# Third filter layer in two 64-row halves, and convolution-tap spectra in 32-row groups, in a diffusion trunk kernel

## Chip, cores and metric

One core of one Trainium2 chip. The metric is the device time of one execution in microseconds (us); lower is better. Engines: TensorE (PE; its weight loads are PEld), VectorE (DVE), ScalarE (ACT), GpSimd (POOL); SyncE (SP) issues most transfers.

## What is computed

Two trunk layers on 128 context tokens and 256 latent tokens of width 1024 in fp32. The parts that matter here are the filters of the long convolution and the taps of the depthwise convolution:

```python
def hyena_filters(L, w1, b1, f1, w2, b2, f2, w3, log_decay):
    ...
    h = jnp.sin(f1 * (z @ w1 + b1))
    h = jnp.sin(f2 * (h @ w2 + b2))
    h = (h @ w3).reshape(L, HYENA_ORDER, 2, HYENA_W)      # third layer: 64 -> 2 orders x 512
    decay = jnp.exp(log_decay).reshape(HYENA_ORDER, 2, HYENA_W)
    h = h * jnp.exp(-tn[:, None, None, None] * decay[None])
    return h * lax.rsqrt(jnp.sum(h * h, axis=(0, 2), keepdims=True) + EPS)

def trunk_layer(x, cond, l, P, cache):
    mod = (silu(cond) @ P['w_mod'][l] + P['b_mod'][l])     # nine modulation vectors
    h = rmsnorm(x, P['g_ffn1'][l]) * (1 + sc1) + sh1
    x = x + 0.5 * g1 * swiglu(h, w1_gate[l], w1_up[l], w1_down[l])
    ...   # attention | 31-tap depthwise convolution | long convolution, then a second swiglu
```

The kernel does both convolutions by spectra, so it needs the spectrum of each filter (two orders) and of the taps (a third spectrum) for each of the two layers.

## The kernel before

All 384 tokens lie in the free dimension. Every large product is split in two parts of reduced precision: a weight block is loaded into a tile `raw` (five buffers), cast to `hi` on ScalarE (L248), its rest `lo` is taken on VectorE (L249), and three matmuls use them (L262 to L264). A block holds eight 128x128 weight tiles, so 24 matmuls. The first feed-forward network of layer 0 runs first: `startup` (L999) is an order written out by hand (`STARTUP`, L43) of modulation starts (M, L286), loads of x (X), the first four columns of the gate and up products (G), the RMS factor (R, and S for its broadcast, L378), and steps of the filter generator (F, L913). After that each gate and up pair j takes one more step of the filter generator until it is used up. Beside that VectorE works off the modulation products (L323), whose weights come through the same `raw` buffers. The order of the instructions on each engine is set by a scheduler when the program is built: it takes what is ready, the earlier in the program first, with some loads and splits raised.

The filter generator makes two sine layers for both trunk layers at once (L916 and L921, 64 rows for each), then `filter_time` for layer 0, `filter_freq` for layer 0, then both for layer 1. In `filter_time` the third layer is a matmul for each order o and time block t (L941): the weights tile `fh` has 128 rows, of which the other layer's 64 are zero, and the moving tile is 128 rows by 512 columns, fp32, into a buffer of the PSUM pool "sp". VectorE multiplies by the decay (L944), combines (L949) and adds squares (L954); ScalarE makes the exponentials (L943) and squares (L953). There are six such steps in a layer, o outside and t inside, a yield after each. In `filter_freq` each spectrum takes three transforms of two matmuls each (`dft`, L637; the matmul is L641), then a butterfly (L645: one ScalarE copy L647, two VectorE operations L648 and L649) and a copy (L985). For the taps the moving tiles have 16, 8 and 8 rows.

The pool "sp" has two buffers; besides the filter steps the RMS sums (L361) and the broadcast of the RMS factor (L381, copied by L383) use it. The scaling of an accumulator by that factor is L413. The PSUM pools "acc" and "S" have two buffers each, and so has "at", which the modulation starts and the sums of squares use.

The attention scores (L810) already use 64-row halves; there a manual dependency and a raised priority keep the two halves of a pair together:

```python
mm = nc.tensor.matmul(S[g], lhsT=st["q"][j][p, b * 128:(b + 1) * 128], rhs=kz[p], start=True,
                      stop=True, tile_position=(64 * g, 0))
if g == 0:
    self.after(mm, read)
```

Of the kernel before, what the change touches and what calls it, by code (L numbers as in the profile page):

```python
# [14 lines left out]
ALU = mybir.AluOpType  # L15
# [176 lines left out]
class Kernel:  # L192
# [720 lines left out]
    def filters(self):  # L913
        nc = self.nc
        p = self.psum("sp")[:, :T]
        nc.tensor.matmul(p, lhsT=self.fw[0:33, 0:128], rhs=self.fz[0:33], start=True, stop=True)  # L916
        h = self.t()
        self.sine(p, 0, 1, [(h, slice(0, 128))])
        yield
        p = self.psum("sp")[:, :T]  # L920
        nc.tensor.matmul(p, lhsT=self.fw[:, 128:256], rhs=h, start=True, stop=True)  # L921
        self.fh = self.S("cv", (128, DEPTH, T))
        nc.gpsimd.memset(self.fh, 0.0)
        self.sine(p, 2, 3, [(self.fh[64 * l:64 * l + 64, l, :], slice(64 * l, 64 * l + 64)) for l in range(DEPTH)])
        yield
        for l in range(DEPTH):
            G = {}
            yield from self.filter_time(l, G)
            yield from self.filter_freq(l, G)

    def filter_time(self, l, G):
        nc = self.nc
        assert "early" in self.loaded
        ssum = self.psum("at")
        for o in range(2):
            dec = self.decay[l, o]
            nc.scalar.activation(out=dec, in_=dec, func=AF.Exp)
            sqs = []
            for t in range(3):
                p = self.psum("sp")  # L940
                nc.tensor.matmul(p, lhsT=self.fh[:, l, t * 128:(t + 1) * 128], rhs=self.fw3[o], start=True, stop=True)  # L941
                h = self.S("P", (128, 512))
                nc.scalar.activation(out=h, in_=dec, func=AF.Exp, scale=self.cst("ntn", t, 1))  # L943
                nc.vector.tensor_tensor(out=h, in0=h, in1=p, op=ALU.mult)  # L944
                if (o, t) == (1, 0):
                    big = self.S("H", (128, 3, 512))
                G[o, t] = g = big[:, t, :] if o else self.S("hy", (128, 512))
                for i in range(2):
                    nc.vector.scalar_tensor_tensor(  # L949
                        out=g[:, i * 256:(i + 1) * 256], in0=h[:, 256:512],  # L950
                        scalar=self.cst("m0", i, 1) if t < 2 else (1.0, -1.0)[i],
                        in1=h[:, 0:256], op0=ALU.mult, op1=ALU.add)
                nc.scalar.activation(out=h, in_=h, func=AF.Square)  # L953
                nc.vector.tensor_tensor(out=h[:, 0:256], in0=h[:, 0:256], in1=h[:, 256:512], op=ALU.add)  # L954
                sqs.append(h)
                if t < 2:
                    yield
            nc.vector.tensor_tensor(out=sqs[1][:, 0:256], in0=sqs[1][:, 0:256], in1=sqs[2][:, 0:256], op=ALU.add)
            for si in range(2):
                for c in range(2):  # L960
                    i = (si * 2 + o) * 2 + c
                    nc.tensor.matmul(ssum[:, i:i + 1], lhsT=sqs[si][:, c * 128:(c + 1) * 128], rhs=self.ones[:, 0:1],
                                     start=True, stop=True)
            yield
        v = self.small(8, "st", 3)
        nc.vector.tensor_scalar(out=v, in0=ssum[:, 0:8], scalar1=EPS, scalar2=None, op0=ALU.add)
        nc.gpsimd.tensor_tensor(out=self.rs[:, 8 * l:8 * l + 8], in0=v, in1=self.mhalf[:, 0:8], op=ALU.pow)

    def filter_freq(self, l, G):
        nc = self.nc  # L970
        cw = [self.S(tag, (16, 768)) for tag in ("cv", "cv", "P")]
        for i in range(2):
            nc.sync.dma_start(out=cw[i], in_=self.d["cw"][l, i])
        nc.vector.tensor_tensor(out=cw[2], in0=cw[0], in1=cw[1], op=ALU.add)
        nc.vector.tensor_tensor(out=cw[0], in0=cw[0], in1=cw[1], op=ALU.subtract)
        rows = (16, 8, 8)
        for o in range(3):
            if o < 2:
                src = [[G[o, t][:, ri * 256:(ri + 1) * 256] for ri in range(2)] for t in range(3)]
            else:  # L980
                src = [[cw[2 - 2 * ri][0:rows[t], t * 256:(t + 1) * 256] for ri in range(2)] for t in range(3)]
            H = self.S("sw", (128, 3, 512))
            U = self.dft(src[2], 2), self.dft(src[1], 1)
            self.butterfly(U[0], U[1], H[:, 2, :], H[:, 1, :])
            nc.scalar.copy(out=H[:, 0, :], in_=self.dft(src[0], 0))  # L985
            nc.gpsimd.dma_start(out=self.Hd[l, o], in_=H)
            yield

# [10 lines left out]
    def startup(self, cols, tags):  # L999
# [5 lines left out]
        for n in STARTUP:  # L1005
# [5 lines left out]
            elif n == "w":  # L1011
                self.fw3 = [self.S("kv", (128, 512)) for _ in range(2)]
                for o in range(2):
                    nc.sync.dma_start(out=self.fw3[o], in_=self.d["hw3"][:, o * 512:(o + 1) * 512])
            elif n == "e":
                self.load_decay(0, ("pt", "pt"))
            elif n == "f":
# [61 lines left out]

def pack_taps(w):  # L1080
    half = CK // 2
    out = np.zeros((DEPTH, 2, 16, 3, 256), np.float32)
    taps = np.zeros((2, half + 1, 256), np.float32)
    for l in range(DEPTH):
        taps[0] = w[l, half::-1]
        taps[1, 1:] = w[l, half + 1:]
        out[l, :, :, 0] = taps
        out[l, :, 0:8, 1] = taps[:, 0::2]
        out[l, :, 0:8, 2] = taps[:, 1::2]
    return out.reshape(DEPTH, 2, 16, 768)  # L1090


def pack_stream(plan, i):
# [50 lines left out]
```

## Time and profile before

| what | value |
|---|---|
| median of three runs | 1521.87 us (1520.0 to 1522.47) |
| the profiled execution | 1519.2 us, span 1517.4 us |
| TensorE busy | 1486.4 us (98%), 8474 instructions |
| VectorE busy | 1116.1 us (74%) |
| ScalarE busy | 671.6 us (44%) |
| mean DMA rate | 171 GB/s |

Busy times are shares of the span. TensorE's matmuls overlap in the record (a matmul of 384 columns is shown as 0.34 us, and the next starts some 0.18 us after it), so a busy TensorE can still lose small amounts between two matmuls; the spacing of the starts tells more than the busy share. An fp32 matmul is recorded as two instructions, so a group of two such matmuls is x4. The chain of waits is followed back from the last instruction of the span, at each step to what released it; "issue" is time in which the engine waited for nothing that the profile shows.

### The profile page before, as it was taken

How to read it: one execution, taken by the hardware profiler on the slowest of the kernel's cores; microseconds unless marked ns; L12 is line 12 of the kernel's file. 1: busy time of each engine (PE TensorE's matmuls, PEld its weight loads, DVE VectorE, ACT ScalarE, POOL GpSimd, SP SyncE). 2: the span in 40 equal slices, each digit the busy share in tenths (PEclk: the TensorE clock that was granted, in tenths of full speed). 3: DMA queues.
4: the chain of work that ended last, by engine and by line, in shares of the span. 5: the costliest groups of instructions: out<-in, count | busy, mean ns of one | idle time of the engine just before them, and what ended most of it. 6: DMA issues, size and time to landing. Idle time of an engine off the chain costs nothing.

```text
span 1517.4 us, 22303 instructions
## 1 busy us (share of the span) xinstructions
PE 1486.4 (98%) x8474; PEld 1416.0 (93%) x8474; DVE 1116.1 (74%) x2120; ACT 671.6 (44%) x1158; POOL 26.8 (2%) x69
## 2 busy tenths in 40 slices
PE   7999999999999999999999999999999999999997
PEld 3799999999978999999999999999996799999997
DVE  5799998886896788896657999755598677555332
ACT  5673333335476553323336333333547665333332
POOL 0101000000000000000000000000000000000000
PEclk9999999999999999999999999999999999999998
DMA  8847777665322357676444777644431234544331
GB/s 281 304 146 257 241 245 235 198 220 174 124 63 70 112 180 222 218 240 196 153 152 125 245 243 246 223 154 155 145 124 36 75 108 156 164 160 154 127 114 42
DMA packets 72059, 259.00 MB, mean 171 GB/s; under 512 B 8144, under 2 KB 9680, under 8 KB 71952
## 3 DMA queue, kind: packets, MB, share of 16 engines
q1 hardware_dynamic: 70832, 252.34, 51.2%
q0 software_dynamic: 1120, 5.24, 1.0%
q8 instruction: 66, 1.08, 0.3%
q14 instruction: 41, 0.34, 0.1%
HBM read 251.00 MB, written 6.55 MB: 170 GB/s over the span
## 4 chain that ended last, share of the span: by engine, by line
PE 74%; DVE 10%; DMA 9%; issue 3%; ACT 2%; SPq 0%; DVEq 0%; POOLq 0%; ACTq 0%
PE acc L262 13%; PE acc L264 13%; PE acc L263 13%; PE S L262 9%; PE S L264 9%; PE S L263 9%; DMA raw<-wmod 9%; DVE junk L323 4%; DVE lo L249 3%; PE sp L641 2%; PE sp L941 1%; PE sp L687 1%; PE S L810 1%; DVE t L502 1%; PE acc L877 0%
## 5 line engine op out<-in xcount | busy, mean ns | idle before, releaser
L249 DVE TENSOR_TENSOR lo<-raw,hi 128x1024 fp32r<-128x1024 f32 x313 | 381.8, 1222 | 182.6 <-ACT hi L248 180.9
L248 ACT CAST hi<-raw 128x1024 fp32r<-128x1024 f32 x313 | 327.3, 1048 | 410.6 <-issue 161.0
L323 DVE SCALAR_TENSOR_TENSOR junk<-raw,cb 128x1024 f32<-128x1024 f32 x256 | 312.7, 1221 | 54.2 <-DMA raw<-wmod 51.7
L262 PE MATMUL acc<-h,hi 128*128 128x384 f32 (+1 forms) x960 | 330.7, 345 | 2.0 <-ACT hi L248 1.6
L264 PE MATMUL acc<-h,lo 128*128 128x384 f32 (+1 forms) x960 | 325.6, 339 | 1.4 <-DVE lo L249 1.3
L263 PE MATMUL acc<-h,hi 128*128 128x384 f32 (+1 forms) x960 | 324.9, 339 | 0.0
L264 PE MATMUL S<-h,lo 128*128 128x384 f32 (+1 forms) x768 | 259.6, 338 | 0.0
L262 PE MATMUL S<-h,hi 128*128 128x384 f32 (+1 forms) x768 | 259.5, 338 | 0.0
L263 PE MATMUL S<-h,hi 128*128 128x384 f32 (+1 forms) x768 | 258.9, 337 | 0.0
L262 PEld LDWEIGHTS acc<-h,hi 128*128 128x128 f32 x960 | 180.5, 188 | 7.5 <-ACT hi L248 2.2
L264 PEld LDWEIGHTS acc<-h,lo 128*128 128x128 f32 x960 | 181.2, 189 | 4.8 <-DVE lo L249 3.0
L263 PEld LDWEIGHTS acc<-h,hi 128*128 128x128 f32 x960 | 180.8, 188 | 3.3 <-issue 1.3
L264 PEld LDWEIGHTS S<-h,lo 128*128 128x128 f32 x768 | 144.7, 188 | 1.2 <-issue 0.8
L262 PEld LDWEIGHTS S<-h,hi 128*128 128x128 f32 x768 | 144.2, 188 | 0.6 <-issue 0.5
L263 PEld LDWEIGHTS S<-h,hi 128*128 128x128 f32 x768 | 144.3, 188 | 0.0
L392 ACT ACTIVATE h<-x,mod 128x128 fp32r<-128x128 f32 x96 | 41.4, 452 | 79.6 <-DVE x L434 78.0
L502 DVE TENSOR_TENSOR t<-S,t 128x384 f32<-128x384 f32 x72 | 39.9, 554 | 33.7 <-PE S L264 33.7
L280 ACT CAST P<-t 128x384 fp32r<-128x384 f32 x24 | 12.3, 513 | 70.5 <-DVE t L502 70.5
L264 PE MATMUL acc<-P,lo 128*128 128x384 f32 x120 | 40.6, 338 | 0.4 <-DVE lo L249 0.4
L262 PE MATMUL acc<-P,hi 128*128 128x384 f32 x120 | 40.6, 338 | 0.0
L263 PE MATMUL acc<-P,hi 128*128 128x384 f32 x120 | 40.5, 338 | 0.0
L393 DVE SCALAR_TENSOR_TENSOR h<-x,mod,h 128x128 fp32r<-128x128 f32 x96 | 38.4, 414 | 1.2
(345 smaller groups left out, 2225.2 us busy)
## 6 DMA issues: line engine op xcount, KB each, us to landing
raw<-stream SPq DMA_DIRECT2D x313, 512.0 KB, 3.5
raw<-wmod SPq DMA_DIRECT2D x128, 512.0 KB, 4.3
raw<-wms SPq DMA_DIRECT2D x16, 512.0 KB, 6.1
Hd<-sw POOLq DMA_DIRECT2D x6, 768.0 KB, 6.0
H<-Hd SPq DMA_DIRECT2D x6, 768.0 KB, 4.9
x<-x SPq DMA_DIRECT2D x8, 192.0 KB, 5.5
y<-h SPq DMA_DIRECT2D x6, 256.0 KB, 2.6
cb<-crow SPq DMA_DIRECT2D x2, 512.0 KB, 8.5
```

Source lines behind the costliest of these rows:

```text
L248: nc.scalar.copy(out=hi, in_=raw)
L249: nc.vector.tensor_tensor(out=lo, in0=raw, in1=hi.bitcast(F32), op=ALU.subtract)
L262: nc.tensor.matmul(out, lhsT=w[0], rhs=x[0], start=start, stop=False)
L263: nc.tensor.matmul(out, lhsT=w[0], rhs=x[1], start=False, stop=False)
L264: nc.tensor.matmul(out, lhsT=w[1], rhs=x[0], start=False, stop=stop)
L323: nc.vector.scalar_tensor_tensor(out=self.junk, in0=raw, scalar=1.0, in1=self.cb[:, ci, :], op0=ALU.mult, op1=ALU.mult, accum_out=m[:, 2 * ...
L392: nc.scalar.mul(out=hl[:, 0, a:b], in_=self.x[k][:, a:b], mul=sc)
L393: nc.vector.scalar_tensor_tensor(out=hl[:, 1, a:b], in0=self.x[k][:, a:b], scalar=sc, in1=hl[:, 0, a:b].bitcast(F32), op0=ALU.mult, op1=AL ...
L502: nc.vector.tensor_tensor(out=s, in0=up[:, :T], in1=s, op=ALU.mult)
L641: self.nc.tensor.matmul(U[:, ri * 256:ri * 256 + 256], lhsT=self.cst(("fw", t), 128 * ri, 128)[:k], rhs=src[ri], start=True, stop=True)
L687: nc.tensor.matmul(ps[:, t * 128:(t + 1) * 128], lhsT=Y[t][:, k:k + 128], rhs=self.cst(("iv", t), 128 * ri, 128), start=ri == 0, stop=ri == 1)
L810: mm = nc.tensor.matmul(S[g], lhsT=st["q"][j][p, b * 128:(b + 1) * 128], rhs=kz[p], start=True, stop=True, tile_position=(64 * g, 0))
```

## The change

For the third layer, `fh` holds each layer's 64 rows twice, once in rows 0 to 63 and once in rows 64 to 127, and is no longer cleared first. The weights `fw3` are laid out by layer: rows 0 to 63 for order 0, rows 64 to 127 for order 1. Each time block then takes two matmuls of 64 rows at tile positions (0, 0) and (64, 0), emitted one behind the other into two "sp" buffers. The loops change places: t is outside and o inside, and both orders' decays are exponentiated in the first step. The sums of squares of both orders are taken at the end.

For the taps, one tile of 96 rows holds three groups of 32 rows (all taps, even taps, odd taps) with the transform's constants beside them; one transfer loads it instead of two. Sum and difference are two VectorE operations on 96 x 256. The six transforms are emitted as three row groups for each of the two parts, at tile positions (64, 0), (32, 0) and (0, 0), into two "sp" buffers and one "at" buffer.

```diff
         self.fh = self.S("cv", (128, DEPTH, T))
-        nc.gpsimd.memset(self.fh, 0.0)
-        self.sine(p, 2, 3, [(self.fh[64 * l:64 * l + 64, l, :], slice(64 * l, 64 * l + 64)) for l in range(DEPTH)])
+        self.sine(p, 2, 3, [(self.fh[64 * o:64 * o + 64, l, :], slice(64 * l, 64 * l + 64))
+                            for l in range(DEPTH) for o in range(2)])
...
         ssum = self.psum("at")
-        for o in range(2):
-            dec = self.decay[l, o]
-            nc.scalar.activation(out=dec, in_=dec, func=AF.Exp)
-            sqs = []
-            for t in range(3):
-                p = self.psum("sp")
-                nc.tensor.matmul(p, lhsT=self.fh[:, l, t * 128:(t + 1) * 128], rhs=self.fw3[o], start=True, stop=True)
+        sqs = [[], []]
+        for t in range(3):
+            ps = [self.psum("sp") for _ in range(2)]
+            for o, p in enumerate(ps):
+                if t == 0:
+                    nc.scalar.activation(out=self.decay[l, o], in_=self.decay[l, o], func=AF.Exp)
+                half = slice(64 * o, 64 * o + 64)
+                nc.tensor.matmul(p, lhsT=self.fh[half, l, t * 128:(t + 1) * 128], rhs=self.fw3[l][half], start=True,
+                                 stop=True, tile_position=(64 * o, 0))
+            for o, p in enumerate(ps):
                 h = self.S("P", (128, 512))
-                nc.scalar.activation(out=h, in_=dec, func=AF.Exp, scale=self.cst("ntn", t, 1))
+                nc.scalar.activation(out=h, in_=self.decay[l, o], func=AF.Exp, scale=self.cst("ntn", t, 1))
                 nc.vector.tensor_tensor(out=h, in0=h, in1=p, op=ALU.mult)
...
-                sqs.append(h)
-                if t < 2:
+                sqs[o].append(h)
+                if (o, t) != (1, 2):
                     yield
...
     def filter_freq(self, l, G):
         nc = self.nc
-        cw = [self.S(tag, (16, 768)) for tag in ("cv", "cv", "P")]
-        for i in range(2):
-            nc.sync.dma_start(out=cw[i], in_=self.d["cw"][l, i])
-        nc.vector.tensor_tensor(out=cw[2], in0=cw[0], in1=cw[1], op=ALU.add)
-        nc.vector.tensor_tensor(out=cw[0], in0=cw[0], in1=cw[1], op=ALU.subtract)
-        rows = (16, 8, 8)
+        cw = self.S("cv", (96, 768))
+        nc.sync.dma_start(out=cw, in_=self.d["cw"][l])
+        taps = self.S("P", (96, 512))
+        for ri, op in enumerate((ALU.add, ALU.subtract)):
+            nc.vector.tensor_tensor(out=taps[:, ri * 256:ri * 256 + 256], in0=cw[:, 0:256], in1=cw[:, 256:512], op=op)
         for o in range(3):
+            H = self.S("sw", (128, 3, 512))
             if o < 2:
                 src = [[G[o, t][:, ri * 256:(ri + 1) * 256] for ri in range(2)] for t in range(3)]
+                U = self.dft(src[2], 2), self.dft(src[1], 1)
             else:
-                src = [[cw[2 - 2 * ri][0:rows[t], t * 256:(t + 1) * 256] for ri in range(2)] for t in range(3)]
-            H = self.S("sw", (128, 3, 512))
-            U = self.dft(src[2], 2), self.dft(src[1], 1)
+                U = self.psum("sp"), self.psum("sp"), self.psum("at")
+                for ri in range(2):
+                    for u, t in zip(U, (2, 1, 0)):
+                        rows = slice(32 * t, 32 * t + 16)
+                        nc.tensor.matmul(u[:, ri * 256:ri * 256 + 256], lhsT=cw[rows, 512 + 128 * ri:640 + 128 * ri],
+                                         rhs=taps[rows, ri * 256:ri * 256 + 256], start=True, stop=True,
+                                         tile_position=(32 * t, 0))
             self.butterfly(U[0], U[1], H[:, 2, :], H[:, 1, :])
-            nc.scalar.copy(out=H[:, 0, :], in_=self.dft(src[0], 0))
+            nc.scalar.copy(out=H[:, 0, :], in_=self.dft(src[0], 0) if o < 2 else U[2])
             nc.gpsimd.dma_start(out=self.Hd[l, o], in_=H)
```

## Rows read from the trace of the kernel before

**Rows 1.** Windows: stretch and length, busy us of each engine, granted clock, DMA share, GB/s

```profile
31.00:62.00 31.00, 29.38 (x196) 23.27 (x195) 24.80 (x82) 18.48 (x40) 3.92 (x4) 0.94 0.86 306
62.00:72.00 10.00, 10.00 (x43) 7.12 (x41) 6.98 (x14) 7.22 (x12) 1.44 (x2) 1.00 0.72 221
72.00:142.00 70.00, 69.38 (x384) 66.21 (x382) 66.53 (x122) 40.55 (x70) 3.42 (x3) 1.00 0.59 200
142.00:341.00 199.00, 198.17 (x1119) 195.50 (x1118) 175.98 (x290) 67.19 (x93) 1.08 (x2) 1.00 0.72 231
```

**Rows 2.** Chain of waits, 62 to 72 us: start us, us, what

```profile
63.71 1.92 PE sp L641 x8
65.63 0.37 PE acc L262
...
66.36 1.05 PE sp L641 x4
67.41 0.37 PE S L262
...
68.33 0.86 PE sp L941 x2
...
70.71 1.72 PE sp L941 x4
```

**Rows 3.** Timeline of PE, 444 to 446 us: start us, us, engine, line, operation

```profile
444.09 0.33 PE L262 MATMUL acc<-h,hi 128*128 128x386 f32 x1
444.35 0.92 PE L810 MATMUL S<-kv,q 64*128 64x384 f32 x4
445.19 0.44 PE L263 MATMUL acc<-h,hi 128*128 128x386 f32 x1
445.48 0.34 PE L264 MATMUL acc<-h,lo 128*128 128x386 f32 x1
```

**Rows 4.** Chain of waits, a modulation start (four column groups, twice)

```profile
50.38 1.00 PE at L292 x16
51.38 0.37 PE acc L262
```

**Rows 5.** Timeline of all engines, 64 to 72 us

```profile
64.81 0.58 ACT L647 COPY sw<-sp 128x512 f32<-128x512 f32 x1 [0.51 <-PE sp L641]
...
66.47 0.69 DVE L649 TENSOR_TENSOR sw<-sp,sw 128x512 f32<-128x512 f32 x1
...
69.23 0.69 DVE L944 TENSOR_TENSOR P<-P,sp 128x512 f32<-128x512 f32 x1 [2.06 <-PE sp L941]
...
69.87 0.48 ACT L383 COPY rb<-sp 128x384 f32<-128x384 f32 x1 [1.21 <-PE sp L381]
...
70.75 0.55 DVE L413 TENSOR_TENSOR t<-acc,rb 128x384 f32<-128x384 f32 x1
...
71.87 0.74 PE L262 MATMUL acc<-h,hi 128*128 128x386 f32 x1
```

**Rows 6.** Chain of waits, its start on VectorE at 142 us and its end

```profile
142.01 1.05 ACT hi L248
...
143.09 1.22 DVE lo L249
...
340.06 1.15 DVE lo L249
...
341.25 0.44 PE S L264
```

**Rows 7.** The sine's line: count, ns min/median/max, first and last start us

```profile
L905 ACT ACTIVATE cv<-t x2: 520/521/522, 17.7 to 18.3; 64x384 f32<-64x384 f32 x2
```

**Rows 8.** Chain of waits, the first product of the third layer

```profile
18.31 2.08 PE sp L941 x2
```

**Rows 9.** The taps' sum on VectorE: count, ns min/median/max, first and last start

```profile
L974 DVE TENSOR_TENSOR P<-cv,cv x2: 940/940/941, 54.0 to 84.6; 16x768 f32<-16x768 f32 x2
```

**Rows 10.** DMA issues, the taps: count, KB each, median us to landing

```profile
cv<-cw SPq DMA_DIRECT2D x4, 48.0 KB, 8.0
```

More of the change, by code (lines that the diff above doesn't have):

```diff
@@ L954, in filter_time @@
                 nc.vector.tensor_tensor(out=h[:, 0:256], in0=h[:, 0:256], in1=h[:, 256:512], op=ALU.add)
-                sqs.append(h)
-                if t < 2:
+                sqs[o].append(h)
+                if (o, t) != (1, 2):
                     yield
-            nc.vector.tensor_tensor(out=sqs[1][:, 0:256], in0=sqs[1][:, 0:256], in1=sqs[2][:, 0:256], op=ALU.add)
+        for o in range(2):
+            nc.vector.tensor_tensor(out=sqs[o][1][:, 0:256], in0=sqs[o][1][:, 0:256], in1=sqs[o][2][:, 0:256],
+                                    op=ALU.add)
             for si in range(2):
@@ L961, in filter_time @@
                     i = (si * 2 + o) * 2 + c
-                    nc.tensor.matmul(ssum[:, i:i + 1], lhsT=sqs[si][:, c * 128:(c + 1) * 128], rhs=self.ones[:, 0:1],
-                                     start=True, stop=True)
-            yield
+                    nc.tensor.matmul(ssum[:, i:i + 1], lhsT=sqs[o][si][:, c * 128:(c + 1) * 128],
+                                     rhs=self.ones[:, 0:1], start=True, stop=True)
+        yield
         v = self.small(8, "st", 3)
@@ L1013, in startup @@
                 for o in range(2):
-                    nc.sync.dma_start(out=self.fw3[o], in_=self.d["hw3"][:, o * 512:(o + 1) * 512])
+                    nc.sync.dma_start(out=self.fw3[o], in_=self.d["hw3"][o])
             elif n == "e":
@@ L1081, in pack_taps @@
     half = CK // 2
-    out = np.zeros((DEPTH, 2, 16, 3, 256), np.float32)
+    out = np.zeros((DEPTH, 96, 768), np.float32)
     taps = np.zeros((2, half + 1, 256), np.float32)
@@ L1086, in pack_taps @@
         taps[1, 1:] = w[l, half + 1:]
[L1087 to L1090, printed above, removed]
+        for t, part in enumerate((taps, taps[:, 0::2], taps[:, 1::2])):
+            n = part.shape[1]
+            out[l, 32 * t:32 * t + n, 0:512] = part.transpose(1, 0, 2).reshape(n, 512)
+            out[l, 32 * t:32 * t + 16, 512:768] = CST_ARR[0:16, CST["fw", t]:CST["fw", t] + 256]
+    return out
 def pack_stream(plan, i):
@@ L1119 @@
         "hw12": hw12,
-        "hw3": np.ascontiguousarray(i["hy_w3"].reshape(128, 1024)),
+        "hw3": np.ascontiguousarray(i["hy_w3"].reshape(DEPTH, 64, 2, 512).transpose(0, 2, 1, 3).reshape(DEPTH, 128, 512)),
         "ld": i["hy_log_decay"],
```

## The prediction

> **What bounds the kernel now.** I read the windows first, for who is busy in which stretch, then the chain of waits, for what is passed on from one stretch to the next, then the timeline around each edited matmul. Times "at" a number are us from the span's start; "layer 0" and "layer 1" are the two filter networks. TensorE is the busiest engine from 31 us on, at a granted clock near full [rows 1]. But it is not alone: from 72 to 142 us VectorE is busy for 66.53 of 70 us, and from 142 to 341 us for 175.98 of 199 us [rows 1]. The chain shows which of them hands time on. Up to 142 us it runs on TensorE nearly without a break. There it leaves TensorE for a split of one weight block (a ScalarE cast at 142.01, a VectorE subtraction at 143.09), and it stays on VectorE and the modulation transfers until another subtraction at 340.06 lets TensorE go on at 341.25 [rows 6]. So time taken off TensorE before 142 us is passed on only as far as the VectorE and transfer work behind it starts earlier too, and what is taken off TensorE just after 142 us lies beside that work.
>
> **Part 1, the third layer's matmuls as pairs.** Before, each of the 12 products takes 0.86 us at full clock: 0.86 for one at 68.33, 1.72 for two at 70.71 [rows 2]. A 64-row product alone is no shorter, since time goes by the 512 columns; only running side by side gains. The nearest row is the attention scores, pairs of 64-row products of 384 columns. Their neighbours start at 444.09 and, behind the pair, at 445.19 and 445.48; with a normal pace of 0.18 the pair takes (445.48 - 0.18) - (444.09 + 0.18) = 1.03 us [rows 3]. One product of 384 columns is 0.86 x 384/512 = 0.64 us, two in turn are 1.28. So the two do run side by side, and 0.39 us goes to entering and leaving. For 512 columns a pair is 0.86 + 0.39 = 1.25 us against 1.72: 0.47 us gained. The other end: halves that become ready apart run alone, each 0.86 + 0.39, 2.50 for the two, 0.78 lost. I take 1.25, the same form.
>
> On this the Trainium skill differs. TensorE: Matmul & The Clock Gate, section "Part 3: Packing small matmuls", gives a pack the span of one matmul plus about 4 ns for each further tile; by it a pair would be 0.86 us and gain 0.86. TensorEngine Tiling (Array Packing), section "Key Properties", says that a change of the tiling mode drains the engine. The scores' rows bear out the second: 0.39 us is lost around a pair. By the first the three pairs of layer 1 would gain 2.6 us, by the rows 1.4; that would lower rival (1) by 1.2 us, and since the rows speak against it, 0.02 of that rival's chance is for it.
>
> **Where layer 0's pairs lie.** They run from 18 to 31 us, where TensorE waits: the first product takes 2.08 us at 18.31, over twice the 0.86 of later ones [rows 2, 8]. Two buffers of the pool "sp" serve them before and after, and product u+2 needs the VectorE multiply of product u in both orders, so this stays a chain of product, multiply, product. The first pair can overlap: up to 1.7 us earlier for its second half. Against that the sine writes four half tiles instead of two, 0.52 us each [rows 7]: 0.52 us ahead of the second half and 1.04 us for whatever is queued behind on ScalarE (a copy that a modulation product needs, and the exponentials). The POOL memset that goes was off the path. Ends: 2.5 us gained, 1.5 lost; I take 0.5 gained, since from 31 to 62 us the DMA engines are busy for 0.86 of the time [rows 1] and feed the blocks that come next.
>
> **Part 2, spectra of the taps.** Before, six products of 256 columns for each layer: in layer 0 1.92 + 1.05 us, and the block after each group is late by 0.37 - 0.18 = 0.19 us, in all 3.35 us [rows 2]. After, three row groups side by side, twice. The nearest row is the modulation start: four column groups side by side, twice, 256 columns as well, 1.00 us and 0.19 behind it [rows 4]; with an entry of about 0.1 (an estimate from the scores' pair, which starts 0.26 behind its neighbour where 0.18 is the pace [rows 3]) 1.3 us at most, so about 2.1 us are gained. Other end: no overlap, three products in turn, about 0.4 gained (one entry and exit fewer). VectorE: two operations of 0.94 us [rows 9] become two on 256 columns instead of 768, at least 0.3 us each, so up to 1.3 us less for each layer. Transfer: two loads of 48 KB [rows 10] become one of 96 x 768 x 4 = 288 KB; at the 306 GB/s of 31 to 62 us [rows 1] the added 192 KB are 0.64 us of a queue that is nearly full, hidden as long as the load is not needed before 54 us, and at worst 0.64 us on the weight blocks behind it.
>
> **What is late next, layer 0's taps and layer 1's first pair (62 to 72 us).** By TensorE alone the stretch shrinks by 2.1 us (taps) and by 2 x 0.86 + 0.86 - 1.25 = 1.33 us (three products leave it, one pair stays). But its end is the first gate block at 71.87, which waits until VectorE has scaled an accumulator (70.75), which waits for the broadcast of the RMS factor, copied by ScalarE at 69.87 [rows 5]. That broadcast takes an "sp" buffer. After the change the pair holds both buffers: the first is free after the copy of 64.81, the second only after the subtraction at 66.47, so at 67.16 [rows 5]. The broadcast must then wait for the pair's first multiply: 67.16 + 0.69 (its length [rows 5]) = 67.85, + about 0.85 for the broadcast, + 0.48 for the copy, + 0.55 for the scaling and some 0.9 of gaps as now, gives about 70.6 instead of 71.87: **1.2 us** gained, not 3.4. The two products at 70.71 filled the wait for that accumulator; the second pair cannot, its buffers are held.
>
> **After 72 us.** Three products of 0.86 (two at 86, one at 109) become two pairs of 1.25: 0.1 gained. Layer 1's taps (from 142.03 us) gain some 2 us of TensorE, but beside the cast and subtraction of 142.01 to 144.31, from which the chain goes on without TensorE [rows 6]: nothing, at most 1.9.
>
> **Sum.** -0.5 (start) - 1.2 (62 to 72 us) - 0.1 - 0 (layer 1's taps), rounded: -1.7 us. The profiled execution took 1519.2 us (span 1517.4 and 1.8 around it), 2.7 below the median of the runs shown, 1521.87; it becomes 1517.5, and the median **1520.2**.
>
> **Rivals.** (1) All TensorE time is passed on: nothing else is late, VectorE gives way because its modulation products can slip into its idle 23 us between 142 and 341 us. Then 2.1 + 2.0 (taps), 1.4 (layer 1's pairs) and up to 2 at the start: 5 to 7 us, 1515 to 1517. For: TensorE at 69.38 of 70 us from 72 to 142 us [rows 1]. Against: the broadcast's wait and the VectorE chain above. (2) VectorE and the modulation transfers hold the end of the first feed-forward stage: TensorE waits longer at 341 us for all it gained: 1521 to 1522. For: VectorE at 95% from 72 to 142 us [rows 1], the wait at 341.25 [rows 6]. Against: VectorE itself gets up to 2.6 us less to do. (3) Slower: the halves don't meet. Both buffers come free at different times (65.4 and 67.16 in the case above [rows 5]), and nothing ties the second half to the first as in the scores, so the scheduler may put weight blocks between them. If four or more of the six pairs are apart, each costs 0.78 instead of gaining 0.47; three in layer 1 make 2.3 us, the sine 1.0, the larger load 0.6, and the broadcast behind a late half another 1 to 2, against 1.2 from the taps: +4, 1526.
> The Trainium skill has the mechanism of the held buffers as a warning: TensorEngine Tiling (Array Packing), "Gotcha 1: PSUM Pressure", says that row tiles need banks of their own and so more of them. By the rows above that costs here the 1.72 us that the two products filled; in rival (3) it decides.
>
> **How the numbers follow.** Forecast 0.43; rival (1) 0.32; rival (2) 0.10; rival (3) 0.15. A measurement of this kernel can tell about 0.2%, 3 us, from no change. The forecast and (2) lie within that, apart from their edges: faster 0.36, same 0.47, slower 0.17. The forecast's own range is 1518 to 1522; to hold 8 in 10 the range takes in most of (1) and reaches toward (3): 1515.5 to 1524.5.
>
> **What would show it.** Pairs: third-layer products in groups of four records within about 1.1 us, the neighbours some 1.25 us apart; with a weight block between the halves rival (3) holds. Taps: one group of twelve records in about 1.1 us, not 1.92 and 1.05. The first gate block of layer 0 at about 70 us; if at 68 or 69, rival (1). A longer TensorE wait near 340 us would be rival (2). What would make it wrong most easily is the order: the scheduler places all instructions anew, and a different order of casts and subtractions in the first 150 us can move more than any term here.

## Result and the profile after

The changed kernel took 1529.77 us (median of 14 runs, 1525.93 to 1537.27), the kernel before 1517.65 on the same chip (14 runs, 1513.06 to 1522.47): a ratio of 1.0080, 95% interval 1.0065 to 1.0094. It is 12 us slower, where 1.7 us faster was forecast, and outside the range. The profiled execution shown here took 1537.27 us (span 1535.5), the longest of the 14.

The windows of the changed kernel, beside [rows 1] (same columns):

```profile
31.00:62.00 31.00, 29.18 (x170) 19.82 (x171) 21.74 (x75) 15.51 (x34) 3.90 (x3) 0.98 0.76 271
...
142.00:341.00 199.00, 195.23 (x1111) 192.33 (x1109) 173.14 (x285) 65.33 (x93) 1.07 (x2) 1.00 0.71 231
```

Two things differ. From 31 to 62 us 26 fewer matmul instructions are done (170 against 196): the kernel is behind before its first feed-forward stage is well under way. And from 142 to 341 us TensorE idles for 3.77 us where it idled for 0.83, although from 149 us on TensorE has the same instructions in the same order as before.

**The start.** Timeline of TensorE in the changed kernel, the third layer of layer 0 (L942) and the first feed-forward block (L262), beside [rows 2, 8], and then the first feed-forward block of the kernel before:

```profile
16.63 2.62 PE L942 MATMUL sp<-kv,cv 64*128 64x512 f32 x4 [0.52 <-ACT cv L905]
...
20.81 2.07 PE L942 MATMUL sp<-kv,cv 64*128 64x512 f32 x2
...
33.65 0.69 PE L262 MATMUL acc<-h,hi 128*128 128x386 f32 x1
```

```profile
31.23 0.53 PE L262 MATMUL acc<-h,hi 128*128 128x386 f32 x1
```

One pair runs together (four records, 16.63). The other four halves run alone, with modulation starts between them, 2.07 us each. The first feed-forward matmul starts at 33.65, where the kernel before had it at 31.23. The lengths are long for every kind of product here: the feed-forward matmuls from 34.14 to 36.07 take 0.53 us, and from 37.52 on 0.34, as in the kernel before from 31.60 on. So TensorE ran at its lower clock until about 37 us (the granted-clock column reads 1.00 there all the same; see the last section). e3_third, below, shows what this means for the start.

The chain of waits of the changed kernel carries that on (start us, us, what):

```profile
49.15 9.27 DMA Hd<-sw
...
58.50 0.59 ACT sw L647
...
60.27 0.62 PE at L991 x2
...
63.77 0.86 PE at L991 x2
...
70.36 1.39 PE sp L991 x8
```

The first finished spectrum is stored at 49.15 (at 44.20 before), and the next one needs the same single "sw" buffer: ScalarE waits for the store until 58.50, and TensorE idles 1.78 us before its next product, at 59.14. The taps (L991) of layer 0 are then not one group but three: the products that go to "at" alone, twice, and the eight records to "sp" only when both its buffers are free. Together 0.62 + 0.86 + 1.39 = 2.87 us, against 1.92 + 1.05 before [rows 2].

Timeline of TensorE from 72 us, beside [rows 5]:

```profile
72.09 1.12 PE L942 MATMUL sp<-kv,cv 64*128 64x512 f32 x2
...
74.63 1.12 PE L942 MATMUL sp<-kv,cv 64*128 64x512 f32 x2
...
75.68 0.91 PE L381 MATMUL sp<-t,ones 128*128 128x384 f32 x2
...
77.24 1.13 PE L942 MATMUL sp<-kv,cv 64*128 64x512 f32 x4
```

Layer 1's first pair is apart too, and the broadcast of the RMS factor (L381) waits behind its halves for an "sp" buffer. The gate block that began at 71.87 begins at 78.56: 6.7 us late. The second pair is together (77.24), the third apart again (101.88 and 105.92 in the chain, 1.05 each). Layer 1's taps do run as one group, twelve records from 147.94 to 149.07, where the kernel before took from 142.03 to 145.01: 1.9 us gained, so that the changed kernel is 4.1 us late at its 440th feed-forward matmul (146.4 us in the kernel before).

**The later stretches.** TensorE's order is that of the kernel before from 149 us on, VectorE's from 259 us on, and still 14 us more are lost by the end of this profile. The page's groups, first of the kernel before, then of the changed kernel (busy us, mean ns | idle time just before them, what ended most of it):

```profile
L323 DVE SCALAR_TENSOR_TENSOR junk<-raw,cb 128x1024 f32<-128x1024 f32 x256 | 312.7, 1221 | 54.2 <-DMA raw<-wmod 51.7
...
L264 PE MATMUL acc<-h,lo 128*128 128x384 f32 (+1 forms) x960 | 325.6, 339 | 1.4 <-DVE lo L249 1.3
```

```profile
L323 DVE SCALAR_TENSOR_TENSOR junk<-raw,cb 128x1024 f32<-128x1024 f32 x256 | 312.8, 1222 | 69.3 <-DMA raw<-wmod 66.7
L264 PE MATMUL acc<-h,lo 128*128 128x384 f32 (+1 forms) x960 | 328.2, 342 | 7.9 <-DVE lo L249 7.8
```

VectorE waits 15 us longer for modulation weights (L323), and TensorE 6.5 us longer for subtractions (L249) that stand behind those products in VectorE's queue. This one group of waits is about half of the 14 us. They lie mainly in the three stretches where modulation products run beside a feed-forward stage (142 to 345, 545 to 700, 880 to 1000 us). The reading that the halved kernels test below: in each, TensorE starts ahead of VectorE by a reserve of finished weight blocks, uses it up, and then moves at the pace of a circle: transfer, two products, subtraction, free buffer, next transfer.

### The profile page after: what moved, and what is told of

Read it like the earlier page. It is cut to its first block, busy times and chain, and to the rows that moved or that the text cites. A ratio compares the mean times of both kernels' runs of the same rounds, so it can differ in the third digit from the quotient of the medians.

```text
span 1535.5 us, 22299 instructions
## 1 busy us (share of the span) xinstructions
PE 1498.0 (98%) x8474; PEld 1415.7 (92%) x8474; DVE 1115.2 (73%) x2120; ACT 671.1 (44%) x1160; POOL 26.5 (2%) x68
## 4 chain that ended last, share of the span: by engine, by line
PE 67%; DMA 13%; DVE 13%; issue 4%; ACT 3%; SPq 0%; DVEq 0%; POOLq 0%; ACTq 0%
DMA raw<-wmod 12%; PE acc L262 12%; PE acc L263 12%; PE acc L264 12%; PE S L262 8%; PE S L263 8%; PE S L264 8%; DVE junk L323 5%; DVE lo L249 4%; PE sp L641 2%; DVE t L502 1%; PE sp L942 1%; PE sp L687 1%; PE S L810 1%; DMA Hd<-sw 1%
## 5 line engine op out<-in xcount | busy, mean ns | idle before, releaser
L249 DVE TENSOR_TENSOR lo<-raw,hi 128x1024 fp32r<-128x1024 f32 x313 | 382.1, 1223 | 179.5 <-ACT hi L248 177.6
L323 DVE SCALAR_TENSOR_TENSOR junk<-raw,cb 128x1024 f32<-128x1024 f32 x256 | 312.8, 1222 | 69.3 <-DMA raw<-wmod 66.7
L264 PE MATMUL acc<-h,lo 128*128 128x384 f32 (+1 forms) x960 | 328.2, 342 | 7.9 <-DVE lo L249 7.8
L262 PE MATMUL acc<-h,hi 128*128 128x384 f32 (+1 forms) x960 | 331.3, 345 | 1.7 <-ACT hi L248 1.2
L262 PE MATMUL S<-h,hi 128*128 128x384 f32 (+1 forms) x768 | 260.1, 339 | 0.0
L264 PE MATMUL S<-h,lo 128*128 128x384 f32 (+1 forms) x768 | 259.2, 338 | 0.1
L264 PEld LDWEIGHTS acc<-h,lo 128*128 128x128 f32 x960 | 181.4, 189 | 16.2 <-DVE lo L249 13.6
L262 PEld LDWEIGHTS acc<-h,hi 128*128 128x128 f32 x960 | 181.3, 189 | 10.6 <-issue 6.3
L264 PEld LDWEIGHTS S<-h,lo 128*128 128x128 f32 x768 | 144.7, 188 | 0.5 <-DVE lo L249 0.4
L262 PEld LDWEIGHTS S<-h,hi 128*128 128x128 f32 x768 | 144.8, 189 | 0.2
L264 PE MATMUL acc<-P,lo 128*128 128x384 f32 x120 | 40.6, 338 | 0.3 <-DVE lo L249 0.3
L262 PE MATMUL acc<-P,hi 128*128 128x384 f32 x120 | 40.6, 338 | 0.0
```

The costliest lines, as they stand in the source:

```text
L249: nc.vector.tensor_tensor(out=lo, in0=raw, in1=hi.bitcast(F32), op=ALU.subtract)
L262: nc.tensor.matmul(out, lhsT=w[0], rhs=x[0], start=start, stop=False)
L264: nc.tensor.matmul(out, lhsT=w[1], rhs=x[0], start=False, stop=stop)
L323: nc.vector.scalar_tensor_tensor(out=self.junk, in0=raw, scalar=1.0, in1=self.cb[:, ci, :], op0=ALU.mult, op1=ALU.mult, accum_out=m[:, 2 * ...
```

## Experiments

Two measures are used throughout. The ratio to the kernel before comes from runs on one chip; levels differ between chips, so times are compared within a group. The lateness of a profiled execution is read from its timeline: the start of the n-th of the 7512 feed-forward matmuls (L262 to L264), minus that start in the profile of the kernel before. A table of it stands behind the last group. Its rows come from several chips, whose levels for the kernel before go from 1517.65 to 1525.03 us, and from one execution each, so it tells where time is lost more than how much.

Theory A at first: the halves issued apart keep TensorE at its lower clock and delay the start, and the rest follows from that. Theory B: the taps tensor, grown from 192 to 576 KB, moves the weights behind it in memory, and their transfers become slower. Theory C: the taps' groups wait for buffers and hold up the start.

### Each part alone, the tensor's size alone, the halves tied

e1_third has the kernel before with only Part 1 (`filter_time`, the sine's four writes, the two layouts of "hw3"), e1_taps with only Part 2 (`filter_freq` and `pack_taps`). e1_pad has no changed instruction:

```diff
-            nc.sync.dma_start(out=cw[i], in_=self.d["cw"][l, i])
+            nc.sync.dma_start(out=cw[i], in_=self.d["cw"][l, i, 0:16])
-    return out.reshape(DEPTH, 2, 16, 768)
+    pad = np.zeros((DEPTH, 2, 48, 768), np.float32)
+    pad[:, :, 0:16] = out.reshape(DEPTH, 2, 16, 768)
+    return pad
```

e1_tied is the changed kernel with the halves held together:

```diff
+                with self.tc.high_priority(offset=PAIR * o):
+                    mm = nc.tensor.matmul(p, ..., tile_position=(64 * o, 0))
+                if o == 0:
+                    self.after(mm, read)
...
-                nc.vector.tensor_tensor(out=h, in0=h, in1=p, op=ALU.mult)
+                read = nc.vector.tensor_tensor(out=h, in0=h, in1=p, op=ALU.mult)
```

> The kernel before with the third layer's 64-row halves alone; the taps' spectra are as before. Theory A (the halves are issued apart while the filters of layer 0 run, so each takes as long as a whole product, the array stays at its slow clock, and the start of the feed-forward work is late): this part carries the larger share, 5 to 10 us slower than before; the first product of the feed-forward network starts 2 us or more later than before (31.2 us there, 33.6 in the changed kernel). Theory B (the larger taps tensor moves the weights in DRAM and makes the modulation transfers slower): within 2 us of before, since nothing moves. Theory C (the taps' spectra in three row groups wait for buffers and hold up the start): within 2 us of before.

> The kernel before with the taps' spectra in 32-row groups alone; the third layer is as before. Theory A: within 3 us of before, either way. Theory B: 5 to 10 us slower, with transfers of modulation weights that land 0.1 us later on average. Theory C: 5 to 10 us slower, of which 3 or more are lost before 150 us.

> The kernel before, with the taps tensor in DRAM padded to the changed kernel's size (rows that no transfer reads); every instruction and its order are those of before. Theory B: 5 us or more slower. Theories A and C: the same within 2 us.

> The changed kernel, with the two halves of a pair tied as the attention scores tie theirs: the first half waits until the second one's buffer is free, and the second has a raised priority. Theory A: the halves of layer 0 run side by side, a pair takes about as long as one half did (2.1 us at the slow clock), the first feed-forward product starts at 32 us or earlier, and the kernel is 2 to 6 us faster than the changed one (about 1524 to 1527). Theories B and C: within 2 us of the changed kernel (1528 to 1532).

Measured: before 1525.03 us; e1_third 1528.09 (1.0016, 0.9996 to 1.0036), e1_taps 1527.51 (1.0014, 1.0001 to 1.0027), e1_pad 1530.31 (1.0036, 1.0018 to 1.0054), e1_tied 1529.61 (1.0029, 1.0015 to 1.0042). Timeline of TensorE of e1_tied (the third layer is L944 there):

```profile
22.56 1.71 PE L944 MATMUL sp<-kv,cv 64*128 64x512 f32 x4
...
27.66 1.13 PE L944 MATMUL sp<-kv,cv 64*128 64x512 f32 x4 [0.56 <-DVE P L951]
28.72 0.44 PE L262 MATMUL acc<-h,hi 128*128 128x386 f32 x1
```

Tied, layer 0's pairs all run together (layer 1's first pair is still apart), and the first feed-forward matmul starts at 28.72 instead of 33.65, as A said. Whether the tie itself did that is taken up with e3_third. The third layer alone cost 3.1 us where A expected 5 to 10, and the padded kernel 5.3 us where only B expected a loss. And the tied kernel was no faster than the padded one, whose instructions are those of the kernel before: something is lost that no instruction carries. e1_taps won 4.8 us up to 146 us of its profile and had given them back by 371 us. B was left as a suspicion: an effect of 0.36% in one loading of one program may be chance.

### Is it chance; does the place matter

e2_null is the kernel before once more, e2_after the changed kernel once more. e2_padlast adds a chunk of zeros at the end of the stream tensor. e2_lay is the changed kernel with the condition rows grown by what the old taps took, and the new taps declared last:

```diff
-        "cw": pack_taps(i["conv_dw"]),
-        "crow": np.concatenate([i["c_ctx"][None], i["c"]], axis=0),
+        "crow": np.concatenate([i["c_ctx"][None], i["c"], np.zeros((48, D), np.float32)], axis=0),
...
     d["stream"] = nc.dram_tensor("stream", ...)
+    arrays["cw"] = pack_taps(i["conv_dw"])
+    d["cw"] = nc.dram_tensor("cw", (DEPTH, 96, 768), ...)
...
     arrays["stream"] = pack_stream(k.plan, i)
```

> The kernel before, unchanged, as a second copy beside itself: how far apart two loadings of one program lie. Theories A (start-up) and B (place of the weights in memory): 0.999 to 1.001 of the kernel before, as the instructions, the order and the addresses are the same. Theory N (each loading of a program draws its own level, and the 1.0036 of the padded kernel was such a draw): 1.002 or more off 1, on either side.

> The changed kernel, unchanged, once more, so that the experiments have it on their own chip. A: its modulation transfers and start-up are what they were, 1.006 to 1.009 of the kernel before; at 150 us of its profile the feed-forward matmuls are 4 us late, as in the first profile. N: anything from 1.002 to 1.009, since the three kernels with one part each stood at 1.0014 to 1.0036.

> The changed kernel with its larger taps tensor declared after all weights, and the tensor of the condition rows grown by as many bytes as the old taps had (its rows 2 to 49 are not read), so that the modulation and stream weights lie where they lay before the change; the instructions and their order are those of the changed kernel. B: the 0.36% of the padded kernel go, 1.002 to 1.005. A: no gain, 1.006 to 1.009, as the halves and the late start are the same.

> The kernel before with one more chunk of zeros (512 KB, not read) at the end of the weight stream: memory grows as in the padded kernel, but no weight moves. B: 0.999 to 1.001. N: up to 0.4% off on either side, as the padded kernel was.

Measured: before 1519.04 us; e2_null 1518.74 (1.0004, 0.9990 to 1.0017), e2_padlast 1517.87 (0.9993, 0.9979 to 1.0006), e2_after 1535.48 (1.0100, 1.0073 to 1.0127), e2_lay 1532.15 (1.0092, 1.0070 to 1.0115). A second loading of one program stands where the first stood, so the 1.0036 was no chance of that kind, and memory that grows behind the weights costs nothing. e2_lay spoke against B, but its tensors were declared in one order and passed in another: the taps were declared after the stream weights and passed ahead of them, so the stream weights may have moved all the same. A trace does not show addresses. That was mended in e3_last.

### The modulation circle taken out

Half of each modulation product is left out in four kernels, so that the circle no longer binds:

```diff
-            raw = self.raw(self.d["wmod"][l, 8 * (3 * sub + kind) + k])
+            raw = self.raw(self.d["wmod"][l, 8 * (3 * sub + kind) + k, :, 0:512], 512)
-            nc.vector.scalar_tensor_tensor(out=self.junk, in0=raw, ..., in1=self.cb[:, ci, :], ...)
+            nc.vector.scalar_tensor_tensor(out=self.junk[:, 0:512], in0=raw[:, 0:512], ..., in1=self.cb[:, ci, 0:512], ...)
```

> The kernel before with every modulation product cut to 512 of its 1024 columns: the 128 modulation weight blocks are loaded and multiplied half only, the other half of each product is left out. Theory R (reserve: TensorE runs ahead of VectorE and the modulation transfers in three stretches, 142 to 345, 545 to 700 and 880 to 1000 us, uses up its reserve of finished weight blocks there and then waits): TensorE has no wait for a subtraction (L249) after 200 us, and the time falls by what those waits cost before, 2 to 7 us (ratio 0.995 to 0.999). Theory S (the late loss of the changed kernel comes from its own transfers or placement): the same for this kernel.

> The changed kernel with the same half of the modulation work left out. R: only its start-up is left, 3 to 5 us over the halved kernel before (the 4 us that its profile was late at 150 us), and the curve of starts against the halved kernel before is flat after 150 us. S: 10 to 16 us over it, growing after 150 us, as the whole kernels stood apart.

> The kernel before with only the taps' spectra in 32-row groups, and the same half of the modulation work left out. R: the gain that its profile showed at 150 us (4.8 us) is kept to the end, 3 to 5 us under the halved kernel before. S: 1 to 3 us over it, as the whole kernel was.

> The kernel before with only the third layer in 64-row halves, and the same half of the modulation work left out. R: its start-up loss (6.7 us at 150 us) is kept, 5 to 8 us over the halved kernel before: more than the 2.4 us of the whole kernel, since there the waits of the three stretches took part of it. S: 1 to 4 us over it, as the whole kernel was.

Measured: before 1521.69 us; h_before 1514.27 (0.9949, 0.9931 to 0.9967), h_after 1519.86 (0.9978, 0.9960 to 0.9996), h_taps 1511.66 (0.9933, 0.9913 to 0.9954), h_third 1520.63 (0.9978, 0.9959 to 0.9997). Against h_before, by the medians, the change costs 5.6 us, the third layer alone 6.4, and the taps alone gain 2.6. Three of the four lie just outside R's ranges (h_before 7.4 us under the kernel before where 2 to 7 were expected, 5.6 and 2.6 where 3 to 5 were), but the three that tell R from S lie near R. In h_after's page TensorE no longer waits for subtractions: the same group L264 has 0.0 us of idle time before it. Its lateness against h_before does not grow behind 146 us (9.1 there, 9.7 from 371 us on, 8.1 at the end). So theory R holds: the start loses some 5 us by the medians, all of it by the third layer, and what the whole kernel loses beyond that is lost where the circle binds. Why it binds harder was still open. The start's loss is no fixed amount either: h_third's twelve times go from 1511.93 to 1523.28 us, h_before's six from 1512.85 to 1515.81. Window of h_third, 20 to 36 us (columns as in [rows 1]):

```profile
20.00:36.00 16.00, 15.51 (x52) 5.34 (x51) 10.26 (x38) 8.99 (x17) 0.00 (x0) 0.50 0.60 209
```

Here the granted clock is on record, 0.50, the lower of its two levels (1.2 GHz of 2.4), and the halves issued alone take the 2.07 us that they take in the changed kernel.

### The weights put back

e3_after is the changed kernel, e3_pad the padded kernel, e3_third Part 1 alone, each once more, on one chip. e3_last is e2_lay with the taps last in both orders:

```diff
     d["stream"] = nc.dram_tensor("stream", ...)
+    d["cw"] = nc.dram_tensor("cw", (DEPTH, 96, 768), ...)
...
     arrays["stream"] = pack_stream(k.plan, i)
+    arrays["cw"] = pack_taps(i["conv_dw"])
```

> The changed kernel once more, as the measure on this chip for the three beside it. Both theories: 1.007 to 1.011 of the kernel before.

> The changed kernel with its taps tensor declared and passed after all others, the stream weights too, and the condition rows grown by the bytes of the old taps, so that every other tensor keeps its old offset if memory is given out in either of these orders. Theory P (place: what the changed kernel loses beyond its start-up comes from where the weights lie): the start-up's 5.6 us and a little more stay, 1.003 to 1.006. Theory Q (the later stretches lose by themselves once the start-up is late): as the changed kernel beside it, 1.007 to 1.011.

> The kernel before with its taps tensor padded to the size that it has after the change, once more and on another chip; no instruction differs. P: again 1.002 to 1.005. Q: 0.999 to 1.001, and the 1.0036 of the first time was that loading or that chip.

> The kernel before with only the third layer in 64-row halves, on one chip with the changed kernel; no tensor changes its size. P: its start-up alone, and less where the three stretches would have waited anyway, 1.001 to 1.005. Q: 1.006 or more, since the halved kernels had shown the start-up of this part to be the later one of the two (6.4 us).

Measured: before 1518.09 us; e3_after 1533.78 (1.0102, 1.0083 to 1.0121), e3_last 1522.22 (1.0032, 1.0014 to 1.0050), e3_pad 1527.87 (1.0075, 1.0055 to 1.0094), e3_third 1526.88 (1.0053, 1.0034 to 1.0072). The same instructions in the same order are 11.6 us faster when the taps tensor stands behind the weights, and the kernel before is 9.8 us slower when its taps tensor is padded ahead of them (more than P's range). In the profiles, e3_after loses 11.8 us behind 146 us and e3_last 1.3, after starts that are equally slow. The page's group L264 shows it, first in e3_after, then in e3_last, then in e3_pad:

```profile
L264 PE MATMUL acc<-h,lo 128*128 128x384 f32 (+1 forms) x960 | 327.9, 342 | 7.7 <-DVE lo L249 7.6
```

```profile
L264 PE MATMUL acc<-h,lo 128*128 128x384 f32 (+1 forms) x960 | 327.0, 341 | 1.1 <-DVE lo L249 0.9
```

```profile
L264 PE MATMUL acc<-h,lo 128*128 128x384 f32 (+1 forms) x960 | 326.9, 341 | 6.1 <-DVE lo L249 6.1
```

Theory B holds so far as the inputs can show it: of 15.7 us on this chip 11.6 go with the taps tensor's place among the inputs, and 4.1 are left. That it works by moving the weights is inferred from the order of the inputs; no trace shows an address.

e3_third's 1.0053 lies between P and Q, but its profile settles something else. It is the same program as e1_third, and every engine has its instructions in the same order in both profiles. Timeline of TensorE, first e1_third, then e3_third: the last half of layer 0, issued alone in both, and the first feed-forward matmul:

```profile
32.28 2.07 PE L942 MATMUL sp<-kv,cv 64*128 64x512 f32 x2
34.29 0.69 PE L262 MATMUL acc<-h,hi 128*128 128x386 f32 x1
```

```profile
27.61 1.12 PE L942 MATMUL sp<-kv,cv 64*128 64x512 f32 x2
28.71 0.44 PE L262 MATMUL acc<-h,hi 128*128 128x386 f32 x1
```

Both begin with long products (2.62 us for the first pair); in e3_third they are short from 21.39 us on, in e1_third from about 38 us. With the halves apart at the higher clock, the feed-forward work starts 2.5 us earlier than in the kernel before, as early as in e1_tied, and at 142 us it is level with the kernel before (0.1 us early), where e1_third is 6.7 us late. So issuing the halves apart does not by itself delay the start; the clock that rises 16 us later does. The two go together: the first feed-forward matmuls take 0.53 us in eight of the nine profiles with untied halves and 0.34 in all eleven others. Why the clock rises at 21 us in one execution and after 36 us in most was not tried.

### Any move, or its alignment; the taps alone

e4_2mb is the kernel before with 512 rows added to the condition rows, so that the weights move by 2 MB where the padded taps moved them by 384 KB. e4_taps_last is e1_taps with the taps tensor last, as in e3_last:

```diff
-        "crow": np.concatenate([i["c_ctx"][None], i["c"]], axis=0),
+        "crow": np.concatenate([i["c_ctx"][None], i["c"], np.zeros((512, D), np.float32)], axis=0),
```

> The kernel before with the tensor of the condition rows grown by 2 MB of rows that are not read, ahead of the modulation and stream weights: these move by four of their 512 KB blocks, where the padded kernel moved them by 384 KB. If the time hangs on how a block lies against a power of two up to 2 MB: 0.999 to 1.001. If any move of the weights, or the greater size ahead of them, costs it: 1.003 to 1.008.

> The kernel before with only the taps' spectra in 32-row groups, and the taps tensor after all others, so that the weights stay where they were. Theory P (place): the start-up gains 2.6 us as in the halved kernels, and up to 2.4 us of that are eaten where TensorE's reserve at 150 us is that much smaller: 0.998 to 1.000 of the kernel before. Theory Q (the later stretches lose by themselves): 1.001 to 1.003, as the same part with the weights moved.

Measured: before 1519.56 us; e4_2mb 1519.58 (1.0003, 0.9987 to 1.0019), e4_taps_last 1516.20 (0.9987, 0.9972 to 1.0002). An input ahead of the weights that is 2 MB larger costs nothing, so it is not any growth ahead of them. That the time hangs on where the blocks lie against some power of two up to 2 MB fits this, but is not shown: it takes for granted that the weights did move by 2 MB. The same group waited 1.2 us for subtractions in e4_2mb.

In the profiles of whole kernels that line sorts them, all but e2_lay: where the taps tensor grew ahead of the weights, TensorE waited 5.7 to 9.1 us for subtractions (the changed kernel three times, the padded one twice, e1_taps, e1_tied); where it did not, 0.3 to 2.6 us (the kernel before, e2_null, e2_padlast, both of the third layer alone, e3_last, both of this group). e2_lay stood between, with 3.1, at a time of 1.0092; what it lost was not traced further. The taps alone, with the weights in place, are the best of all whole kernels here, 3.4 us under the kernel before by the medians, but the interval still touches 1.

Lateness against the profile of the kernel before, in us (columns: the n of the feed-forward matmul, and its start in the kernel before):

```
              0: 31.2  140: 80.1  440: 146.4  1700: 371.3  3400: 724.2  5200: 1040.4  7500: 1504.2
e2_null         -0.4      -0.4        +1.1         +2.0         -1.0          -0.5          -0.4
e4_2mb          -2.1      -0.5        -0.4         +1.4         -0.4          +1.4          -0.3
e3_pad          -0.5      -1.2        -0.5         +1.1         +2.9          +8.5          +8.5
after           +2.4      +6.4        +4.1         +8.3        +10.9         +16.3         +17.9
e3_after        +3.4      +5.5        +3.1         +7.9         +8.7         +14.9         +14.9
e3_last         +3.3      +8.4        +5.6         +7.5         +4.4          +6.9          +6.9
e2_lay          +2.5      +5.9        +3.2         +3.8         +5.7         +11.3         +11.2
e1_third        +3.1      +7.3        +6.7         +7.1         +6.1         +12.6         +12.5
e3_third        -2.5      +0.8        +1.5         +2.9          0.0          +2.5          +2.4
e1_taps         -1.2      -3.1        -4.8         -0.2         +2.2          +8.4          +8.5
e4_taps_last    -0.9      -3.0        -4.6         -4.3         -4.8          -2.1          -3.6
e1_tied         -2.5      +3.2        -0.7         +5.8         +6.9         +13.5         +15.0
```

To 146 us the rows differ by their instructions and by when the clock rose (e1_third against e3_third); behind it mainly by the place of the taps tensor: compare, on one chip, e3_after with e3_last and e4_2mb with e3_pad. e1_taps and e4_taps_last show the same, but on two chips. e1_third is the exception: no tensor of it changed its size, and it loses 6.5 us between 724 and 1040 us all the same, part of it where its clock reads 0.66 from 969 to 974 us. The rest is open; on its chip the kernel before is slower too, 1525.03 us.

## Why the prediction was wrong

**The bound.** Its reading was right: the stretch from 142 us belongs to VectorE and the modulation transfers. It was used only to say where gains stop. That a loss can start there, if a transfer lands a little later, was not asked: the durations of the transfers were taken as given.

**The larger load.** This step failed by the most. It priced 192 KB more for each load, "at worst 0.64 us", as bytes in a queue. What cost 11.6 us (e3_last against e3_after) and 9.8 us (e3_pad against the kernel before) on one chip, and 5.3 us (e1_pad) on another, is that the tensor grew ahead of the weights, most likely because that moved them. No rival held it.

**Where layer 0's pairs lie.** This is the other step that failed. It took 0.5 us gained, with 1.5 lost as the other end; the first feed-forward matmul came 2.4 us late in this profile, and 3.4 in e3_after's. The working read that the first product takes 2.08 us, "over twice the 0.86 of later ones", and gave no term to when that pace ends. With the halves untied it ended after 36 us in eight of nine profiles, in the kernel before by 25 us; in e3_third, where it ended at 21 us, the halves were just as far apart and the start was 2.5 us early. "The first pair can overlap" came true for that pair alone; the other halves were issued apart.

**62 to 72 us.** 1.2 us gained was forecast, a gate block at 70.6; it came at 78.56. The held buffers were rightly named, and the broadcast did wait behind the pair's multiply. But most of the lateness had come before: 4.95 us at the first store of a spectrum, and the wait of the next one for the single "sw" buffer, which the working did not name at all. Before, that wait was 0.17 us on ScalarE.

**The prices of a pair.** 1.25 us was forecast for a pair and for each half apart. By the same spacing of the neighbours' starts e1_tied's pair at 98.13 takes (99.47 - 0.18) - (97.86 + 0.18) = 1.25 us, and the half alone at 101.81 in the changed kernel (103.14 - 0.18) - (101.55 + 0.18) = 1.23. These terms were right; whether the halves would meet was the question. By the rule of the Trainium skill (TensorE: Matmul & The Clock Gate, section "Part 3: Packing small matmuls") a pair would have been about 0.86 us, an estimate; the trace's 1.25 fits the drain at a change of mode that the Trainium skill's TensorEngine Tiling (Array Packing), section "Key Properties", states. As recorded, the pair takes 1.13 us (77.24) and a half alone 1.12 (72.09): the second tile itself adds next to nothing.

**The taps.** In layer 0 2.1 us were forecast and 0.1 came, since the groups waited for buffers and split. In layer 1 some 2 us of TensorE were forecast, and 1.9 came. That nothing of it would be passed on is not settled: the taps alone were 3.4 us under the kernel before with the weights in place (an interval that touches 1), and 2.5 us over it on another chip with the tensor grown ahead of them.

**The rivals.** Rival (3) came true in its condition: four of the six pairs are apart. Its price was +4; measured were +4.1 with the weights in place (e3_last) and +5.6 with the circle taken out (h_after). That the sizes agree is in part luck: the rival had no term for the clock, and in e3_third, where the clock rose early, the halves apart had cost nothing by 142 us. It had a chance of 0.15, though the text itself says that nothing ties the halves together: that was reason enough to give its condition more. With e3_last's ratio alone the changed kernel would have stood near 1517.65 x 1.0032 = 1522.5, inside the range. Rival (2) fits e1_taps, whose gain was gone between 146 and 371 us; e4_taps_last kept its gain there (-4.6 and -4.3).

## What to carry to other kernels

Before two small products are paired, ask when each one's buffer comes free: if not at the same time and nothing ties them, each runs alone at nearly the price of the pair (1.23 us against 1.25 here). Before an early delay is put down to the order of the work, compare the lengths of like instructions: here one order had two starts, 5.6 us apart, by the clock. And where a stage is held by transfers, the size of any input ahead of the weights can be a change of that stage; put grown inputs last, or time the kernel before with the input padded, which separates the two at once.

## Not expected of the hardware

- A taps tensor 384 KB larger ahead of the weights cost the kernel before 5.3 us on one chip and 9.8 on another, with no compute instruction changed; condition rows 2 MB larger ahead of them, or 512 KB more behind them, cost nothing. In the stretch from 880 to 1000 us the modulation blocks land in a median of 4.5 us in e3_after, 4.4 in e3_pad, 4.3 in e3_last and 4.2 in e4_2mb, all on one chip. This median alone does not tell the kernels apart: it is 4.3 in e2_after, which waited 5.7 us for subtractions, and 4.5 in e1_third, which waited 2.6. The circle repeats every 9 us (VectorE's waits for such a block end at 886, 895, 904 and 913 us in e2_after). What in the memory makes the difference was not tried.
- The granted clock in the windows reads 1.00 from 16 to 36 us in the changed kernel, yet a half product takes 2.07 us there and 1.12 at 101.81. In h_third the column reads 0.50 from 20 to 36 us with the same lengths. In that stretch the length of like instructions told the pace, and the changed kernel's column did not. From 60 to 64 us, behind the 1.78 us idle before 59.14, the column does read 0.60.
- Part 1 alone cost 1.0016 on one chip and 1.0053 on another (intervals that just overlap), and 6.4 us with the circle taken out. e1_third and e3_third show one reason: the same order of instructions with the clock rising after 36 us, or at 21 us.
